# Hyena convolutions over even and odd pairs of positions, with half the matrix products, and weights whose low part a DMA adds up

## The chip, the cores and the metric

The kernel runs on one core of one Trainium2 chip. The core has a matrix engine (TensorE, PE in the rows), VectorE (DVE), ScalarE (ACT), GpSimd (POOL), SyncE (SP) and DMA engines that move data between HBM and the on-chip memory (SBUF). Matrix products are written to PSUM, eight banks of 128 x 512 floats. The metric is the time of one execution on the device in microseconds, the median of several runs. A profile is one execution taken by the hardware profiler.

## The reference, cut to what matters

One layer of an encoder: a combined input projection (2048 to 11264 columns), four groups of 1024 channels (convolution, Fourier mixing, Hyena long convolutions, attention over a memory), a gate, an output projection. The change is in the Hyena group:

```python
hy = depthwise_conv(hy, hy_short_w, hy_short_b)      # width 3
v, x1, x2 = jnp.split(hy, 3, axis=-1)
kf = hyena_filters(...)                              # spectra, (L+1, 2, 1024)
z = v
for o, g_o in enumerate((x1, x2)):
    z = g_o * long_conv(z, kf[:, o], hy_skip[o])     # zero-padded FFT convolution, L = 512
y_c = z
```

So there are 8 blocks of 128 channels with 2 long convolutions each, 16 in all; the second of a block takes the result of the first.

## The kernel before, in words

**Precision.** Every product is in float32 made from rounded parts. A matrix is split into a high part (rounded to fp32r) and a low part (what is left), and `mm3` (L102) issues three matmuls: high x high, high x low, low x high. `split` (L77) makes the parts: ScalarE copies the source into the high part (L79), VectorE subtracts it from the source (L80).

**Projection weights.** `project` (L304) computes one block of 128 output columns: 2 chunks of 1024 weights per partition, 24 matmuls of 512 columns each. `wload` (L98) loads a chunk (512 KB, from SyncE's queue) into `raw`, ScalarE writes `wh`, VectorE writes `wl`. `raw`, `wh` and `wl` have three buffers each, so the parts of a chunk can be written when the products of the chunk three earlier are done.

**The Hyena stage** (loop at L608). For each of 8 blocks `ct`: three projections with the short convolution (`short`, L535) give `v`, `x1` and `x2`; two `long_conv` (L546) follow; in four of the blocks there are also two projections for the convolution group (`conv_proj`) and 30 multiply-adds on VectorE over the positions (`conv_taps`, L516).

**One long convolution before.** Sums and differences of even positions and reversed odd positions (`pq`, L553 and L554), 4 transposes (L558), a split (`tH`, `tL`), the forward transform as products with two 256 x 256 tables (`mtab`; 24 matmuls of 256 columns), the product with the filter's spectrum (`kt_`, loaded from `kd`) as 4 multiplications and 2 sums on VectorE, two splits (`uH`, `uL`, `vH`, `vL`), the inverse transform (24 matmuls of 256 columns, that leave the positions on the free axis), scaling, skip term and gate.

**What sets the order.** The program is written with a tile framework: when it is built, a scheduler takes instructions by priority and by its own estimate of times and lays down one fixed order for each engine, so matmuls of the next projections stand between those of a convolution. On the chip each engine runs its list in order, and an instruction whose input or buffer isn't ready holds up all behind it. GpSimd's list has only additions (L476 for sums of squares, L520 for channel sums) in this stage.

Of the kernel before, what the change touches and what calls it, by code (L numbers as in the profile page):

```python
# [20 lines left out]
P = 128  # L21
# [21 lines left out]
def encoder_kernel(ctx: ExitStack, tc: tile.TileContext, a: dict, out: bass.AP):  # L43
# [26 lines left out]
    def pg():  # L70
        return psg.tile([P, 512], F32, tag="pg", name=nm("pg"))
# [463 lines left out]
    def short(b, j):  # L535
        ps = project(b)
# [6 lines left out]
    MH = [mtab[:, 0, i, :].rearrange("p (s r) -> p s r", s=2) for i in range(2)]  # L543
    ML = [mtab[:, 1, i, :].rearrange("p (s r) -> p s r", s=2) for i in range(2)]

    def long_conv(z, g, dst, o, ct):  # L546
# [17 lines left out]
        pu, px = pg(), pg()
        for m, pst in ((0, pu), (1, px)):
            for rt in range(2):
                o_ = pst[:, 256 * rt:256 * rt + 256]
                for st in range(2):
                    s = slice(P * rt, P * rt + P)
                    if m == 0:  # L570
                        xh, xl = tHv[:, st], tLv[:, st]
                    else:
                        xh, xl = tHv[:, st, ::-1, :], tLv[:, st, ::-1, :]
                    mm3(o_, MH[m][:, st, s], ML[m][:, st, s], xh, xl, st == 0, st == 1)
        puv = pu.rearrange("p (r c n) -> p r c n", r=2, c=2)
        pxv = px.rearrange("p (r c n) -> p r c n", r=2, c=2)
        kc, ks = kt_[:, :, 0:2, :], kt_[:, :, 2:4, :]
        uH, uL, vH, vL = (wt(t, (P, 2, 2, P), F32R, 1) for t in ("uH", "uL", "vH", "vL"))
        for yh, yl, k1, k2, op in ((uH, uL, kc, ks, add), (vH, vL, ks, kc, sub)):
            p1 = wt("pp", (P, 2, 2, P), bufs=3)  # L580
            p2 = wt("pp", (P, 2, 2, P), bufs=3)
            dve.tensor_tensor(p1, puv, k1, op=mul)
            dve.tensor_tensor(p2, pxv, k2, op=mul)
            if op == add:
                dve.tensor_tensor(p1, p1, p2, op=add)  # L585
            else:
                dve.tensor_tensor(p1, p2, p1, op=sub)
            split(yh, yl, p1)
        pd = pg()

        for f in range(2):
            o_ = pd[:, 256 * f:256 * f + 256]
            n = 0
            for m, yh, yl, c in ((0, uH, uL, f), (1, vH, vL, 1 - f)):
                for rt in range(2):
                    mm3(o_, yh[:, rt, c, :], yl[:, rt, c, :], MH[m][:, rt, :], ML[m][:, rt, :], n == 0, n == 3)
                    n += 1
        ci = cinv[:, o, ct:ct + 1]
        dsb = wt("dsb", (P, 256))
        act.activation(dsb, pd[:, 256:512], AF.Copy, scale=ci)  # L600
        yc = wt("yc")
# [6 lines left out]
    for ct in range(CT):  # L608
# [7 lines left out]
        group_square(y, gacc, wt("pp", (P, 2, 2, P), bufs=3).rearrange("p a b c -> p (a b c)"), ct == 0)  # L616
# [552 lines left out]
```

## Time and profile before

| | |
|---|---|
| median of 3 runs | 1731.67 us (1730.17 to 1737.29) |
| profiled execution | 1736.26 us, of which 1734.0 us from its first to its last instruction (the span) |
| TensorE busy | 1687.0 us, 97% of the span; granted clock 0.987 of 2.4 GHz on the mean |
| VectorE, ScalarE, GpSimd busy | 1205.5, 752.3 and 151.4 us |
| DMA | 215.13 MB, mean 124 GB/s |

A matmul's row gives its start and its length; the lengths overlap, so the rate of TensorE is read from the distance of the starts. "Idle before" is the time in which an engine stood still ahead of a group of instructions, with what ended it. The Hyena stage lies between about 320 and 790 us of the span.

### The profile page before, as it was taken

The numbers are of one execution on the slowest core, as the hardware profiler recorded it, in microseconds if no ns is written. First come the engines' busy times: TensorE is split into PE (matmuls) and PEld (weight loads), VectorE is DVE, ScalarE is ACT, GpSimd is POOL, SyncE is SP. The second block draws the span as 40 slices with busy tenths as digits, with TensorE's granted clock in tenths as the row PEclk, the third lists the DMA queues.
The fourth block names the chain that finished last, engine by engine and source line by source line (L and its number), as shares of the span: only waits on it lengthen the run. The fifth ranks groups of instructions, "written<-read, shape, count | busy, mean of one in ns | idle before, by whom it ended". The sixth has DMA issues, their size and how long they took to land.

```text
span 1734.0 us, 22272 instructions
## 1 busy us (share of the span) xinstructions
PE 1687.0 (97%) x8521; PEld 1424.7 (82%) x8521; DVE 1205.5 (70%) x1755; ACT 752.3 (43%) x1121; POOL 151.4 (9%) x98
## 2 busy tenths in 40 slices
PE   7999999999999999999999999999999699999997
PEld 5987888888888888888888898888878588888876
DVE  7966988478587686878765879986462545454586
ACT  6645655232223222223434346445453444444564
POOL 4201432000000000000000011100021100000000
PEclk9999999999999999999999999999999899999999
DMA  8654443432222322223333234232222523232355
GB/s 285 226 186 150 158 146 134 158 95 88 98 93 90 97 98 91 77 82 116 128 116 128 94 117 158 98 109 86 74 85 97 200 98 104 98 103 98 117 206 182
DMA packets 80575, 215.13 MB, mean 124 GB/s; under 512 B 8146, under 2 KB 25810, under 8 KB 79956
## 3 DMA queue, kind: packets, MB, share of 16 engines
q1 hardware_dynamic: 80468, 213.70, 36.5%
q8 instruction: 67, 1.10, 0.3%
q14 instruction: 40, 0.33, 0.1%
HBM read 195.05 MB, written 18.63 MB: 123 GB/s over the span
## 4 chain that ended last, share of the span: by engine, by line
PE 87%; DVE 7%; issue 2%; ACT 2%; DMA 2%; POOL 1%; SPq 0%; DVEq 0%; ACTq 0%; POOLq 0%
PE pf L105 16%; PE pf L103 16%; PE pf L104 16%; PE pg L103 12%; PE pg L104 12%; PE pg L105 12%; DVE y L516 2%; DVE wl L80 2%; DMA raw<-in_wv_dram 1%; POOL vacc L476 1%; ACT wh L79 1%; DMA kdm<-mst 0%; PE pg L558 0%; DVE y L491 0%; PE pg L411 0%
## 5 line engine op out<-in xcount | busy, mean ns | idle before, releaser
L103 PE MATMUL pf<-hH,wh 128*128 128x512 f32 x1280 | 504.7, 394 | 0.0
L105 PE MATMUL pf<-hH,wl 128*128 128x512 f32 x1280 | 502.1, 392 | 0.0
L104 PE MATMUL pf<-hL,wh 128*128 128x512 f32 x1280 | 501.5, 392 | 0.0
L80 DVE TENSOR_TENSOR wl<-raw,wh 128x1024 fp32r<-128x1024 f32 (+1 forms) x288 | 359.1, 1249 | 187.0 <-ACT wh L79 185.8
L79 ACT ACTIVATE wh<-raw 128x1024 fp32r<-128x1024 f32 (+1 forms) x288 | 298.3, 1037 | 358.9 <-PE pf L104 275.8
L103 PEld LDWEIGHTS pf<-hH,wh 128*128 128x128 f32 x1280 | 241.8, 189 | 47.7 <-issue 0.8
L105 PEld LDWEIGHTS pf<-hH,wl 128*128 128x128 f32 x1280 | 241.5, 189 | 47.4 <-issue 0.5
L104 PEld LDWEIGHTS pf<-hL,wh 128*128 128x128 f32 x1280 | 241.4, 189 | 47.2 <-issue 0.2
L80 DVE TENSOR_TENSOR jl<-y,jh 128x512 fp32r<-128x512 f32 (+1 forms) x154 | 91.5, 597 | 121.2 <-ACT jh L79 120.1
L79 ACT ACTIVATE jh<-y 128x512 fp32r<-128x512 f32 (+1 forms) x154 | 84.5, 550 | 179.3 <-PE pg L104 113.0
L103 PE MATMUL pg<-wh,jh 128*128 128x512 f32 x384 | 150.5, 392 | 11.2 <-ACT jh L79 11.2
L104 PE MATMUL pg<-wl,jh 128*128 128x512 f32 x384 | 150.2, 391 | 0.0
L105 PE MATMUL pg<-wh,jl 128*128 128x512 f32 x384 | 150.1, 391 | 0.0
L103 PEld LDWEIGHTS pg<-wh,jh 128*128 128x128 f32 x384 | 72.6, 189 | 26.4 <-ACT jh L79 11.5
L516 DVE SCALAR_TENSOR_TENSOR y<-ubuf,par,y 128x512 f32<-128x512 f32 x120 | 89.8, 748 | 2.5
L105 PEld LDWEIGHTS pg<-wh,jl 128*128 128x128 f32 x384 | 72.5, 189 | 15.4 <-DVE jl L80 0.2
L104 PEld LDWEIGHTS pg<-wl,jh 128*128 128x128 f32 x384 | 72.7, 189 | 15.1
L79 ACT ACTIVATE uH<-pp 128x512 fp32r<-128x512 f32 x16 | 10.1, 632 | 92.9 <-DVE pp L585 92.9
L516 DVE SCALAR_TENSOR_TENSOR y<-ub,par,y 128x512 f32<-128x512 f32 x60 | 46.4, 773 | 2.3 <-ACT y L514 1.1
L427 POOL TENSOR_TENSOR y<-fsq,y 128x512 f32<-128x512 f32 x24 | 43.6, 1815 | 41.5 <-ACT fsq L426 41.4
L104 PE MATMUL pf<-wl,jh 128*128 128x512 f32 x116 | 45.2, 390 | 1.3 <-DVE wl L80 1.3
L516 DVE SCALAR_TENSOR_TENSOR y<-ubm,par,y 128x512 f32<-128x512 f32 x60 | 45.2, 753 | 0.8
(374 smaller groups left out, 2847.3 us busy)
## 6 DMA issues: line engine op xcount, KB each, us to landing
raw<-in_w_std_dram SPq DMA_DIRECT2D x160, 512.0 KB, 3.8
raw<-in_wo_dram SPq DMA_DIRECT2D x77, 512.0 KB, 3.3
raw<-in_wk_dram SPq DMA_DIRECT2D x16, 512.0 KB, 4.0
kd<-y SPq DMA_DIRECT2D x16, 512.0 KB, 3.5
y<-kd SPq DMA_DIRECT2D x32, 256.0 KB, 3.3
raw<-in_w_f_dram SPq DMA_DIRECT2D x16, 512.0 KB, 3.3
raw<-in_wv_dram SPq DMA_DIRECT2D x15, 512.0 KB, 5.9
y<-in_xT_dram SPq DMA_DIRECT2D x8, 512.0 KB, 6.8
```

The costliest lines, as they stand in the source:

```text
L79: act.activation(h, src, AF.Copy)
L80: dve.tensor_tensor(l, src, h, op=sub)
L103: pe.matmul(ps, wh, xh, start=start, stop=False)
L104: pe.matmul(ps, wh, xl, start=False, stop=False)
L105: pe.matmul(ps, wl, xh, start=False, stop=stop)
L427: pool.tensor_tensor(acc, sq, acc, op=add)
L476: pool.tensor_tensor(acc, sqt, acc, op=add)
L516: dve.scalar_tensor_tensor(o, u[:, t:t + L], conv_w[:, ct, t:t + 1], o, op0=mul, op1=add)
```

## The change: what it does

- `long_conv`: the sums and differences `pq` are taken for even and odd pair indices apart (positions in steps of four), the forward transform uses two 128 x 128 tables for each of the two (12 matmuls of 256 columns), and sums and differences on VectorE build the full spectrum from the two halves. After the product with the filter the same is done backwards, then one split of 1024 elements (`wwH`, `wwL`) in place of two of 512, and 12 matmuls. The result lies with positions on the partitions, so 4 transposes (L624) turn it back. ScalarE copies one half out of PSUM at L584 and L617 and makes the skip term (L626).
- `short` takes its weights by `wload_dma`: ScalarE writes the negated rounded weights into `wl` and the rounded ones into `wh`, and a DMA from GpSimd's queue adds the same 512 KB of HBM onto `wl`. VectorE doesn't touch these chunks. 48 of the chunks are loaded in this way; those of `conv_proj` are as before.
- Several working tiles have one buffer where they had two. Tables change: `mtab` has other values, half the columns of `etab` are doubled, some with their sign turned.

```diff
+    def wload_dma(src):
+        raw = load(src)
+        h, l = wparts()
+        act.activation(l, raw, AF.Copy, scale=-1.0)
+        act.activation(h, raw, AF.Copy)
+        pool.dma_start(l, src, accum_op=add)
+        return h, l
...
-    def project(b, fill=None):
+    def project(b, fill=None, how=wload):
...
-            wh, wl = wload(a["w_std"][b, :, 1024 * c:1024 * c + 1024])
+            wh, wl = how(a["w_std"][b, :, 1024 * c:1024 * c + 1024])
...
-        ps = project(b)
+        ps = project(b, how=wload_dma)
...
-        for m, pst in ((0, pu), (1, px)):
-            for rt in range(2):
...
-                for st in range(2):
...
-                    mm3(o_, MH[m][:, st, s], ML[m][:, st, s], xh, xl, st == 0, st == 1)
+        for e in range(2):
+            v = slice(256 * e, 256 * e + 256)
+            for m in range(2):
+                mm3(pse[e][:, 256 * m:256 * m + 256], MH[:, 0, m, e], ML[:, 0, m, e], tH[:, v], tL[:, v], True, True)
+        odd = wt("pp", bufs=3)
+        act.activation(odd, pse[1], AF.Copy)
+        xy = wt("t1", bufs=1)
+        ab = wt("ab4", (P, 2, 2, 256), bufs=1)
+        dve.tensor_tensor(xy, pse[0], odd, op=add)
+        dve.tensor_tensor(ab[:, :, 1, :], pse[0].rearrange("p (m n) -> p m n", m=2), odd.rearrange("p (m n) -> p m n", m=2), op=sub)
+        dve.tensor_tensor(ab[:, 0, 0, :], xy[:, 0:256], xy[:, 256:512], op=add)
+        dve.tensor_tensor(ab[:, 1, 0, :], xy[:, 0:256], xy[:, 256:512], op=sub)
...
+            dve.tensor_tensor(p1, x1_, k1, op=mul)
+            dve.tensor_tensor(p2, x2_, k2, op=mul)
+            dve.tensor_tensor(uv[:, i_].rearrange("p r (c n) -> p r c n", c=2), p1, p2, op=op)
+        sd = wt("t1", (P, 2, 256), bufs=1)
+        dve.tensor_tensor(sd[:, 0], uv[:, 0, 0], uv[:, 1, 0], op=add)
+        dve.tensor_tensor(sd[:, 1], uv[:, 0, 0], uv[:, 1, 0], op=sub)
+        w_ = wt("ab4", (P, 2, 2, 256), bufs=1)
+        dve.tensor_tensor(w_[:, 0], sd, uv[:, :, 1, :], op=add)
+        dve.tensor_tensor(w_[:, 1], sd, uv[:, :, 1, :], op=sub)
...
+        split(wH, wL, w_)
         pd = pg()
+        for e in range(2):
+            for m in range(2):
+                mm3(pd[:, 256 * e:256 * e + 256], MH[:, 1, m, e], ML[:, 1, m, e], wH[:, e, m], wL[:, e, m], m == 0, m == 1)
...
+        act.activation(dif, pdv[:, 1], AF.Copy)
+        th_ = wt("t1", (P, 2, 2, P), bufs=1)
+        dve.tensor_tensor(th_[:, 0], pdv[:, 0], dif, op=add)
+        dve.tensor_tensor(th_[:, 1], pdv[:, 0], dif, op=sub)
+        pc = pg()
+        for h in range(2):
+            for e in range(2):
+                pe.transpose(pc[:, 256 * h + P * e:256 * h + P * e + P], th_[:, h, e, :], ident)
+        yc = wt("yc", bufs=1)
+        act.activation(yc, z, AF.Copy, scale=skip[:, o, ct:ct + 1])
+        pcv = pc.rearrange("p (h e n) -> p h e n", h=2, e=2)
+        for h, yv in enumerate(pairs(yc)):
+            dve.scalar_tensor_tensor(yv, pcv[:, h], cinv[:, o, ct:ct + 1], yv, op0=mul, op1=add)
         dve.tensor_tensor(dst, yc, g, op=mul)
```

Three places show how the order moves. The first is TensorE's list in the first long convolution, between the last matmul of the forward transform (into `pg_562`) and the first of the inverse. `pf` rows are matmuls of projections; before, the inverse takes `uH`, and 13 projection matmuls stand between:

```order
L105 MATMUL pg_562_3234<-tH_559_3229,mtab_3009 128x256
L104 MATMUL pf_593_3402<-hL_99,wh_595_3405 128x512
L105 MATMUL pf_593_3402<-hH_98,wl_596_3406 128x512
...
L103 MATMUL pf_593_3402<-hH_98,wh_598_3435 128x512
L104 MATMUL pf_593_3402<-hL_99,wh_598_3435 128x512
L103 MATMUL pg_571_3277<-mtab_3009,uH_563_3259 128x256
```

After, the inverse takes `wwH` and `wwL`, and 52 projection matmuls stand at the place of the 13:

```order
L114 MATMUL pg_562_3240<-tH_559_3235,mtab_3009 128x256
L113 MATMUL pf_605_3398<-hL_99,wh_607_3401 128x512
L114 MATMUL pf_605_3398<-hH_98,wl_608_3402 128x512
...
L112 MATMUL pf_612_3460<-hH_98,wh_614_3463 128x512
L113 MATMUL pf_612_3460<-hL_99,wh_614_3463 128x512
L112 MATMUL pg_575_3282<-wwH_573_3278,mtab_3009 128x256
```

In the 16 convolutions there are 43 to 62 projection matmuls at this place.

The second is VectorE's list between these same two points. Before, four multiplications (`pp` from PSUM), two sums and the splits:

```order
L582 TENSOR_TENSOR pp_567_3263<-pg_561_3233,y2_531_3018 128x512
L583 TENSOR_TENSOR pp_568_3264<-pg_562_3234,y2_531_3018 128x512
L582 TENSOR_TENSOR pp_569_3270<-pg_561_3233,y2_531_3018 128x512
...
L585 TENSOR_TENSOR pp_567_3263<-pp_567_3263,pp_568_3264 128x512
L583 TENSOR_TENSOR pp_570_3271<-pg_562_3234,y2_531_3018 128x512
```

After, 14 instructions stand between the forward transform and `wwH` (the first four and the last four of them, then the split's low part):

```order
L587 TENSOR_TENSOR t1_564_3255<-pg_561_3239,pp_563_3253 128x512
L588 TENSOR_TENSOR ab4_565_3256<-pg_561_3239,pp_563_3253 128x2x256
L589 TENSOR_TENSOR ab4_565_3256<-t1_564_3255 128x256
L590 TENSOR_TENSOR ab4_565_3256<-t1_564_3255 128x256
...
L602 TENSOR_TENSOR t1_571_3272<-uv_566_3261 128x256
L603 TENSOR_TENSOR t1_571_3272<-uv_566_3261 128x256
L605 TENSOR_TENSOR ab4_572_3275<-t1_571_3272,uv_566_3261 128x512
L606 TENSOR_TENSOR ab4_572_3275<-t1_571_3272,uv_566_3261 128x512
L80 TENSOR_TENSOR wwL_574_3279<-ab4_572_3275,wwH_573_3278 128x1024
```

The middle six are the four multiplications and two sums, as before in number and size.

The third is GpSimd's list in the middle of the stage, which before held additions alone and now has the 48 transfers among them:

```order
L108 DMA wl_709_4065<-in_w_std_dram 128x1024
L108 DMA wl_712_4096<-in_w_std_dram 128x1024
L485 TENSOR_TENSOR gaccC_3023<-pp_689_3924,gaccC_3023 128x512
L108 DMA wl_779_4462<-in_w_std_dram 128x1024
L108 DMA wl_782_4493<-in_w_std_dram 128x1024
```

## Rows read from the trace of the kernel before

**Rows 1.** The page: busy us, share of the span, instructions of an engine.

```profile
PE 1687.0 (97%) x8521; PEld 1424.7 (82%) x8521; DVE 1205.5 (70%) x1755; ACT 752.3 (43%) x1121; POOL 151.4 (9%) x98
```

**Rows 2.** Busy time of each engine in the Hyena stage, clock, DMA share, GB/s.

```profile
320.00:790.00 470.00, 469.99 (x2441) 394.09 (x2440) 347.09 (x493) 133.34 (x175) 17.10 (x10) 1.00 0.28 92
```

**Rows 3.** Groups on TensorE, 320 to 790 us: busy, mean ns, idle before.

```profile
L104 PE MATMUL pg<-tL,mtab 128*128 128x256 f32 x128 | 35.6, 284 | 0.0
...
L104 PE MATMUL pg<-mtab,vH 128*128 128x256 f32 x64 | 18.1, 282 | 0.0
...
L558 PE MATMUL pg<-ident,pq 128*128 128x128 f32 x64 | 11.1, 276 | 0.0
```

**Rows 4.** TensorE in order of time: start, length, instruction.

```profile
339.26 0.39 PE L105 MATMUL pf<-hH,wl 128*128 128x512 f32 x1
339.49 0.60 PE L558 MATMUL pg<-ident,pq 128*128 128x128 f32 x4
339.85 0.47 PE L103 MATMUL pf<-hH,wh 128*128 128x512 f32 x1
...
343.33 0.28 PE L105 MATMUL pg<-tH,mtab 128*128 128x256 f32 x1
...
345.73 0.28 PE L105 MATMUL pg<-tH,mtab 128*128 128x256 f32 x1
...
365.20 0.39 PE L103 MATMUL pf<-hH,wh 128*128 128x512 f32 x1
...
367.24 0.39 PE L103 MATMUL pf<-hH,wh 128*128 128x512 f32 x1
```

**Rows 5.** Groups on VectorE, 320 to 790 us.

```profile
L80 DVE TENSOR_TENSOR wl<-raw,wh 128x1024 fp32r<-128x1024 f32 x68 | 84.3, 1240 | 44.2 <-ACT wh L79 43.6
...
L582 DVE TENSOR_TENSOR pp<-pg,y 128x512 f32<-128x512 f32 x32 | 22.0, 686 | 17.4 <-PE pg L105 17.4
...
L602 DVE SCALAR_TENSOR_TENSOR yc<-pg,cinv,dsb 128x256 f32<-128x256 f32 x16 | 7.7, 484 | 46.1 <-ACT dsb L600 46.1
...
L553 DVE TENSOR_TENSOR pq<-vx 128x256 f32<-128x256 f32 x8 | 3.4, 422 | 0.1
```

**Rows 6.** Groups on ScalarE, 320 to 790 us.

```profile
L79 ACT ACTIVATE wh<-raw 128x1024 fp32r<-128x1024 f32 x67 | 70.9, 1058 | 169.3 <-PE pf L104 160.4 <-issue 8.8
...
L79 ACT ACTIVATE tH<-pg 128x512 fp32r<-128x512 f32 x16 | 9.5, 591 | 0.2
L600 ACT ACTIVATE dsb<-pg,cinv 128x256 f32<-128x256 f32 x16 | 7.6, 477 | 56.1 <-PE pg L105 56.1
```

**Rows 7.** Waits, 320 to 790 us: who for whom, total us, times, longest.

```profile
PEld pg L103 <- ACT vH L79: 4.1, 15, 0.3
PEld pg L103 <- ACT tH L79: 3.6, 16, 0.3
```

**Rows 8.** DMA, 320 to 790 us: queue's share; issues, KB each, us to landing.

```profile
q1 hardware_dynamic: 23733, 42.76, 27.5%
...
raw<-in_w_std_dram SPq DMA_DIRECT2D x65, 512.0 KB, 3.7
```

**Rows 9.** DMA, 0 to 60 us, the busiest stretch: the slowest 512 KB transfer.

```profile
y<-in_xT_dram SPq DMA_DIRECT2D x8, 512.0 KB, 6.8
```

**Rows 10.** GpSimd's additions: min/median/max ns, first and last start.

```profile
L476 POOL TENSOR_TENSOR gaccC<-pp,gaccC x7: 1296/1305/1764, 443.9 to 782.8; 128x512 f32<-128x512 f32 x7
...
L520 POOL TENSOR_TENSOR csum<-y,csum x6: 1292/2209/2877, 635.2 to 1180.2; 128x512 f32<-128x512 f32 x6
```

**Rows 11.** VectorE in order of time, with taps of the convolution group.

```profile
376.88 4.68 DVE L516 SCALAR_TENSOR_TENSOR y<-ubuf,par,y 128x512 f32<-128x512 f32 x6
381.48 1.22 DVE L80 TENSOR_TENSOR wl<-raw,wh 128x1024 fp32r<-128x1024 f32 x1
382.62 3.89 DVE L516 SCALAR_TENSOR_TENSOR y<-ubuf,par,y 128x512 f32<-128x512 f32 x5
```

More of the change, by code (lines that the diff above doesn't have):

```diff
@@ L541, in short, with pairs @@
         return t
-    MH = [mtab[:, 0, i, :].rearrange("p (s r) -> p s r", s=2) for i in range(2)]
-    ML = [mtab[:, 1, i, :].rearrange("p (s r) -> p s r", s=2) for i in range(2)]
+    MH, ML = (mtab[:, i].rearrange("p (d m e n) -> p d m e n", d=2, m=2, e=2) for i in range(2))
+    def pairs(z):
+        return z[:, 0::2].rearrange("p (i e) -> p e i", e=2), z[:, 511::-2].rearrange("p (i e) -> p e i", e=2)
     def long_conv(z, g, dst, o, ct):
@@ L551, in long_conv @@
             sp.dma_start(kt_[:, rt], kdr[ct // 2][o][:, rt, :, cs])
-        pq = wt("pq")
-        dve.tensor_tensor(pq[:, 0:256], z[:, 0::2], z[:, 511::-2], op=add)
-        dve.tensor_tensor(pq[:, 256:512], z[:, 0::2], z[:, 511::-2], op=sub)
+        z0, z1 = pairs(z)
+        pq = wt("pq", (P, 2, 2, P), bufs=1)
+        dve.tensor_tensor(pq[:, 0], z0, z1, op=add)
+        dve.tensor_tensor(pq[:, 1], z0, z1, op=sub)
         pt = pg()
-        for st in range(2):
+        for e in range(2):
@@ L564, in long_conv @@
-        pu, px = pg(), pg()
-        for m, pst in ((0, pu), (1, px)):
-            for rt in range(2):
[L567 to L573, printed above, removed]
-                    mm3(o_, MH[m][:, st, s], ML[m][:, st, s], xh, xl, st == 0, st == 1)
@@ L577, in long_conv @@
+        dve.tensor_tensor(xy, pse[0], odd, op=add)
+        dve.tensor_tensor(ab[:, :, 1, :], pse[0].rearrange("p (m n) -> p m n", m=2), odd.rearrange("p (m n) -> p m n", m=2), op=sub)
+        dve.tensor_tensor(ab[:, 0, 0, :], xy[:, 0:256], xy[:, 256:512], op=add)
+        dve.tensor_tensor(ab[:, 1, 0, :], xy[:, 0:256], xy[:, 256:512], op=sub)
+        av, bv = (ab[:, i_].rearrange("p r (c n) -> p r c n", c=2) for i_ in range(2))
         kc, ks = kt_[:, :, 0:2, :], kt_[:, :, 2:4, :]
-        uH, uL, vH, vL = (wt(t, (P, 2, 2, P), F32R, 1) for t in ("uH", "uL", "vH", "vL"))
@@ L579, in long_conv @@
-        for yh, yl, k1, k2, op in ((uH, uL, kc, ks, add), (vH, vL, ks, kc, sub)):
+        uv = wt("uv", (P, 2, 2, 256), bufs=1)
+        for i_, (x1_, k1, x2_, k2, op) in enumerate(((av, kc, bv[:, :, ::-1, :], ks, add), (bv, kc[:, :, ::-1, :], av[:, :, ::-1, :], ks[:, :, ::-1, :], sub))):
             p1 = wt("pp", (P, 2, 2, P), bufs=3)
             p2 = wt("pp", (P, 2, 2, P), bufs=3)
[L582 to L588, printed above, removed]
@@ L589, in long_conv @@
-        pd = pg()
[L591 to L601, printed above, removed]
@@ new lines, in long_conv @@
+        dve.tensor_tensor(sd[:, 0], uv[:, 0, 0], uv[:, 1, 0], op=add)
[3 more added lines that the diff above has]
+        dve.tensor_tensor(w_[:, 1], sd, uv[:, :, 1, :], op=sub)
+        wH = wt("wwH", (P, 2, 2, 256), F32R, 1)
+        wL = wt("wwL", (P, 2, 2, 256), F32R, 1)
+        split(wH, wL, w_)
+        pd = pg()
+        for e in range(2):
+            for m in range(2):
+                mm3(pd[:, 256 * e:256 * e + 256], MH[:, 1, m, e], ML[:, 1, m, e], wH[:, e, m], wL[:, e, m], m == 0, m == 1)
@@ new lines, in long_conv @@
+        pdv = pd.rearrange("p (e f n) -> p f e n", e=2, f=2)
+        dif = wt("pp", (P, 2, P), bufs=3)
+        act.activation(dif, pdv[:, 1], AF.Copy)
[4 more added lines that the diff above has]
+        for h in range(2):
+            for e in range(2):
+                pe.transpose(pc[:, 256 * h + P * e:256 * h + P * e + P], th_[:, h, e, :], ident)
@@ L1053, in _tables @@
     i = np.arange(256)
-    th = np.pi * np.outer(4 * i + 1, 4 * i + 1) / 2048.0
-    m = np.stack([np.cos(th) + np.sin(th), np.cos(th) - np.sin(th)])
-    t = {"mtab": m.reshape(2, 2, P, 256).transpose(2, 0, 1, 3).reshape(P, 1024)}
+    j = np.arange(P)
+    m = np.stack([np.stack([f(np.pi * np.outer(8 * j + 4 * e + 1, 4 * j + 1) / 2048.0) for e in range(2)]) for f in (np.cos, np.sin)])
+    t = {"mtab": np.stack([m.transpose(2, 0, 1, 3), m.transpose(3, 0, 1, 2)], axis=1).reshape(P, 1024)}
     phi = np.pi * (4 * i + 1) / 1024.0
     e = np.stack([f(np.outer(2 * i + par, phi)) for f in (np.cos, np.sin) for par in (0, 1)])
+    e[:2, :, P:] *= 2.0
+    e[2:, :, P:] *= -2.0
     t["etab"] = e.reshape(4, 2, P, 256).transpose(2, 0, 1, 3).reshape(P, 2048)
```

20 lines of the change are left out of this document (7 added, 13 removed).

## The prediction

> **What bounds the kernel now.** I read the page first: TensorE is busy for 97% of the span [rows 1], so the question is whether it also works without gaps in the stage that changes. The stretch of the Hyena stage, 320 to 790 us, answers it: TensorE is busy 469.99 of 470.00 us at the full clock (1.00), VectorE 347 us (74%), ScalarE 133 us (28%), GpSimd 17 us, and the DMA engines are in use for 28% [rows 2]. The groups on TensorE show no idle time before them [rows 3], and the waits of its weight loads for ScalarE or VectorE are short: at most 0.3 us each, 4.1 and 3.6 us in all 16 convolutions for the two longest kinds, most of it under a running matmul [rows 7]. So this stage lasts as long as the sum of its matmul steps, and a matmul less is its step less, as long as nothing else becomes late.
>
> **TensorE's sum.** Steps are distances of starts. Projection matmuls of 512 columns: from 365.20 to 367.24 lie 9 steps, 0.227 us each. Matmuls of 256 columns: from 343.33 to 345.73 lie 20 steps, 0.120 us each. Four transposes stand between two projection matmuls that start 0.59 us apart; less one step, 0.36 us, 0.09 us each [rows 4]. The convolutions have 768 matmuls of 256 columns (three lines of 128 forward, six of 64 inverse, one row of each kind shown [rows 3]); the change halves them: 384 x 0.120 = 46.1 us less. It adds 64 transposes, 64 x 0.09 = 5.8 us. Net -40.3 us. The number of projection matmuls stays.
>
> **VectorE.** Durations: 0.69 us for 512 elements, 0.42 for 256 (0.48 from PSUM), 1.24 for 1024 [rows 5]. One convolution gains four instructions of 512 (`xy`, one half of `ab`, two for `w_`: 2.76), four of 256 (1.69), two of 256 from PSUM (0.97), has one split of 1024 for two of 512 (1.24 - 1.37) and loses the skip term, of 512 (0.7; it goes to ScalarE): +4.5 us, 72 us in 16. The 48 subtractions for `wl` go: 48 x 1.24 = 59.5 us. VectorE thus ends with 347 + 13 = 360 us in a stage of about 434 us: 83%. It is not the bound on the mean.
>
> **ScalarE.** 48 more conversions at 1.06 us are 51 us [rows 6]; a convolution has two copies of 512 (0.59 each), one of 256 (0.48) and one of 1024 (1.06) where it had two of 512 and one of 256, about +1 us, 16 us in all. 133 + 67 = 200 us, 46%. No bound either, but it works its list in order, and a conversion that waits for a buffer holds up those behind it.
>
> **The convolution's chain.** From the end of the forward transform to the first inverse matmul lie a ScalarE copy (0.59), ten VectorE instructions of 512 and four of 256 (6.86 + 1.69) and ScalarE's copy into `wwH` (1.06): 10.2 us [rows 5, 6]. Where instructions follow each other, the next starts up to 0.08 us before the end of the one ahead (376.88 + 4.68 against 381.48 [rows 11]); 13 times that takes it down to 9.2. The order puts 43 to 62 projection matmuls there: 9.8 to 14.1 us at 0.227. At the tightest place the chain ends between 0.6 us too early and 0.4 us too late, plus the hand-overs between engines; at the others VectorE has other work in between. Each convolution also has one hand-over more than before (the turn back). The old order, made in the same way, cost next to nothing. I take 0.25 us for each convolution, 4 us in all; the ends are 0 and 0.6 us (10 us).
>
> **The weights by DMA.** The trace of before has no transfer that adds and none from GpSimd. `wl` of a chunk is free when the chunk three earlier is done and needed by the third matmul of its own: two chunks and two matmuls, 50 x 0.227 = 11.3 us at the tightest (11.3 to 14.9 in all but the first three, since convolution matmuls stand between). ScalarE needs two conversions, the first a matmul earlier: 2.1 - 0.2 = 1.9 us. So 9.4 us are left for GpSimd's issue and the transfer at the tightest place, 11 typically. The bounds of its time X: a plain load of the same 512 KB lands 3.7 us after its issue here [rows 8]; the slowest 512 KB transfer, in the busiest stretch, took 6.8 us [rows 9], and since the adding one has to read its destination as well, twice that, 13.6, is the upper end. I take twice the row of this stage, 7.4 us, which fits into 9.4: cost 0. What hides it is the projection matmuls of the two chunks before. The DMA engines carry 25 MB more on 43 [rows 8]: from 27.5% to some 47%, or 64% if the second read costs as much. Nothing comes free of idle by moving 59.5 us from VectorE, since TensorE didn't wait for it.
>
> What is late if X is too long: three buffers turn. An adding chunk holds its buffer for 5.4 (its 24 matmuls) + 1.9 + X, a plain one for 5.4 + 1.06 + 1.24 = 7.7. Two blocks, one of them with the convolution group, have 12 and 4 of these: (12 (X + 7.3) + 4 x 7.7) / 3 = 4X + 39.5 us. TensorE needs for them 16 x 5.44 + 4 x (24 x 0.12 + 8 x 0.09) = 101.4 us. They are equal at X = 15.5, and each us more costs 4 us in each of the four pairs, 16 us in all. At 13.6 the mean still fits, but single tight places run late by up to 4.2 us; a late chunk makes the next two easier, so some 5 us in a pair, 20 us in all.
>
> Behind a transfer on GpSimd stand the later transfers and 10 or so additions. An addition takes 1.3 to 2.2 us, rarely 2.9 [rows 10], and waits for ScalarE's squares or for the last tap; at the tightest place the margin of 9.4 - 7.4 = 2.0 us is about one addition.
>
> **A rule that speaks against it.** GpSimd's addition of 512 elements takes 1.31 us at the median in one group and 2.21 in another, the second right behind VectorE's taps [rows 10]; so the two engines do disturb each other in this kernel. The Trainium skill (SBUF — State Buffer, section "SBUF: two separate sides") says that GpSimd writes the descriptors of the DMAs that it issues, and can't while VectorE holds the pair of ports they share, which single-source float32 copies do; two-input instructions hold it only against reads by GpSimd. By that, the two-input instructions of this stage would not delay a transfer, and the sum stays; read more widely, it is the third rival below.
>
> **Sum.** -46.1 + 5.8 + 4 = -36.3 us. The profiled execution took 1736.26 us (1734.0 of it span), which gives 1700; it lay 4.6 us above the median of 1731.67, and from that the forecast is 1695.
>
> **Rivals.**
> 1. *Adding transfers turn too slowly (slower).* The only place where the change can lose more than it gains is the round of the three `wl` buffers. From X = 17.7 us the delay, 16 X - 248 us, eats the 36 us; at X = 20 it is 72 us, and the time 1732 - 36 + 72 = 1768. For it: no row shows such a transfer, and it is 4.8 times the plain one. Against: even the slowest plain one, doubled, stays at 13.6. Chance 0.12.
> 2. *The longer chain shows.* VectorE at 83% with taps and `wl` subtractions of the other projections in its list delivers `wwH` 1.5 us late in each convolution: 24 us in place of 4, 1715. For it: 43 matmuls cover barely 10.2 us, and 14 dependent steps stand where there were 4. Against: before, the same kind of order lost at most 0.3 us at a hand-over [rows 7]. The same time comes out if X is near 13 us. Chance 0.15.
> 3. *GpSimd can't issue while VectorE is busy (no change).* VectorE runs 9.6 us without a pause among the taps (376.88 to 386.51 [rows 11]). If the issue waits for the end of such a run, X is 7.4 + 9.6 = 17 there, 7.6 us too late, once or twice in each of the four blocks with taps: 30 to 61 us. That is 1726 to 1756, with 1731 as the likeliest, no gain. Chance 0.07.
>
> **How the numbers follow.** Forecast 0.66 (1688 to 1706: from 0 to 10 us of hand-overs, and some us of the runs' own spread), rivals 0.12, 0.15 and 0.07. A difference under 0.5%, 8.7 us, can't be told from no change. Faster by more than that (below 1723): the forecast, nearly all of rival 2: 0.80. Within it: most of rival 3 and a little of the others: 0.07. Slower (above 1740): rival 1 and a part of 3: 0.13. The range goes from 1687 to 1735; above it lies rival 1 and half of rival 3, some 0.16, below it 0.03. The forecast's own range is 1688 to 1706.
>
> **What would show it.** Right: in the stage (then some 434 us long) TensorE without idle time and at clock 1.00, 384 matmuls of 256 columns left of 768, 128 transposes, and `wl` transfers that land within 9 us of ScalarE's conversion. Wrong: `pf` matmuls with idle time released by the `wl` DMA (rivals 1 and 3; in 3 only beside taps), or `pg` matmuls with idle time released by `wwH`, `wwL` or `t1` (rival 2); or a clock below 1.00 in the stage, which would come from such pauses.

## The result, and the profile after

The changed kernel takes 1715.51 us in the median of 4 runs (1713.90 to 1717.04), the kernel before, on the same chip, 1733.12 us (1730.17 to 1737.29). The ratio is 0.9894, with a 95% interval of 0.9877 to 0.9911: 18 us less, half of the 36 us that were forecast. The profiled execution took 1716.29 us, 1714.5 of it span (1734.0 before).

The page's first line, in answer to [rows 1]: busy us, share of the span, instructions.

```profile
PE 1655.3 (97%) x8201; PEld 1386.6 (81%) x8201; DVE 1221.9 (71%) x1835; ACT 813.6 (47%) x1185; POOL 189.9 (11%) x146
```

TensorE's share of the span is 97% as before. The stage itself says more. Busy time, clock, DMA share and GB/s, in answer to [rows 2]:

```profile
320.00:766.00 446.00, 436.04 (x2109) 353.28 (x2108) 357.08 (x554) 186.73 (x228) 51.27 (x52) 1.00 0.63 150
...
500.00:600.00 100.00, 96.92 (x474) 77.79 (x472) 80.10 (x128) 41.57 (x52) 12.78 (x13) 1.00 0.66 152
```

TensorE stood idle for 10 of 446 us, where it was busy for 469.99 of 470; the pauses lie all over the stage, and the clock stays full in it. Starts show more than busy time does, since a row's length overlaps the next: from start to start, less the usual step (0.227, 0.120 or 0.091 us), TensorE lost 7.8 us between 300 and 795 us before the change and 24.8 us between 300 and 760 us after it. What it waited for stands in the waits (us in all, times, longest), in answer to [rows 7]:

```profile
PEld pg L113 <- DVE tL L80: 9.9, 14, 1.9
...
PE pg L113 <- DVE tL L80: 4.9, 6, 1.5
PEld pg L112 <- ACT wwH L79: 4.7, 15, 0.6
...
PE pg L573 <- DVE pq L568: 4.4, 8, 0.6
```

Two places cost: the transposes of `pq` (L573; 8.3 us by the starts) and the first matmul that needs `tL` (L113; 6.5 us). The place on which the prediction spent its argument, `wwH`, costs 1.0 us by the starts, most of its wait lying under running matmuls.

The turn from the first convolution of a block to the second, on TensorE and VectorE in order of time (start, length, instruction, idle before):

```profile
358.57 0.69 PE L624 MATMUL pg<-ident,t 128*128 128x128 f32 x4
359.01 0.48 PE L112 MATMUL pf<-hH,wh 128*128 128x512 f32 x1
...
359.30 1.29 DVE L629 SCALAR_TENSOR_TENSOR yc<-pg,cinv,yc 128x256 f32<-128x256 f32 x2 [0.53 <-PE pg L624]
...
360.62 0.69 DVE L630 TENSOR_TENSOR y<-yc,vx 128x512 f32<-128x512 f32 x1
...
361.17 0.39 PE L112 MATMUL pf<-hH,wh 128*128 128x512 f32 x1
361.35 0.63 DVE L568 TENSOR_TENSOR pq<-y 128x256 f32<-128x256 f32 x1
...
361.89 0.63 DVE L569 TENSOR_TENSOR pq<-y 128x256 f32<-128x256 f32 x1
...
362.03 0.33 PE L573 MATMUL pg<-ident,pq 128*128 128x128 f32 x1 [0.47 <-DVE pq L568]
362.11 0.48 PE L113 MATMUL pf<-hL,wh 128*128 128x512 f32 x1
362.58 0.55 PE L573 MATMUL pg<-ident,pq 128*128 128x128 f32 x3
```

VectorE works from 359.30 to 362.52 without a gap: it isn't waiting, its instructions last 3.2 us. TensorE has ten projection matmuls for that time, 2.27 us, and loses some 0.9 us at each of the eight such places. In the order before the change, 16 projection matmuls stood between two convolutions at each of these places, and the next transposes started 3.83 us after the last inverse matmul did: the new order also has less to cover this turn. In answer to [rows 5], VectorE's groups there (busy, mean ns of one, idle before):

```profile
L629 DVE SCALAR_TENSOR_TENSOR yc<-pg,cinv,yc 128x256 f32<-128x256 f32 x30 | 19.2, 688 | 6.5 <-PE pg L624 6.3
...
L589 DVE TENSOR_TENSOR ab<-t 128x256 f32<-128x256 f32 x16 | 6.7, 416 | 0.0
...
L568 DVE TENSOR_TENSOR pq<-y 128x256 f32<-128x256 f32 x8 | 5.0, 628 | 0.3
```

All three have 256 elements. `ab`, contiguous, takes 416 ns; `pq`, whose sources step by four floats, 628, where its ancestor with steps of two took 422 [rows 5]; `yc`, read and written in steps of four, 688 for 484.

The second place, in a block with taps:

```profile
510.18 0.49 PE L112 MATMUL pg<-tH,mtab 128*128 128x256 f32 x2
...
511.48 0.74 DVE L548 SCALAR_TENSOR_TENSOR vx<-pf,par,vx 128x511 f32<-128x511 f32 x1
...
512.81 0.74 DVE L549 SCALAR_TENSOR_TENSOR vx<-pf,par,vx 128x511 f32<-128x511 f32 x1
...
513.47 0.68 DVE L80 TENSOR_TENSOR tL<-pg,tH 128x512 fp32r<-128x512 f32 x1
...
514.20 0.39 PE L113 MATMUL pg<-tL,mtab 128*128 128x256 f32 x1 [1.46 <-DVE tL L80]
```

`tL` could start when `tH` was there (TensorE takes it at 510.18), but stands in VectorE's list behind taps and a short convolution that are themselves late. Three such pauses are 1.7 to 1.9 us long from start to start.

A third loss lies behind the stage, where the next one begins:

```profile
780.47 0.36 PE L112 MATMUL pg<-jh,wh 128*128 128x258 f32 x1 [1.21 <-issue]
...
786.04 0.39 PE L112 MATMUL pg<-jh,wh 128*128 128x258 f32 x1 [1.65 <-ACT wh L79]
```

From 10 us ahead of the first `jh` matmul to 26 us behind it the pauses (steps at least 0.15 us longer than usual) add up to 4.2 us; before, to 0.2.

The transfers, in answer to [rows 8], between 300 and 766 us:

```profile
q0 software_dynamic: 6586, 23.96, 27.9%
...
raw<-in_w_std_dram SPq DMA_DIRECT2D x67, 512.0 KB, 4.7
wl<-in_w_std_dram POOLq DMA_DIRECT2D x45, 512.0 KB, 7.8
```

An adding transfer lands 7.8 us after its issue at the median (6.7 to 9.7); in the whole stage TensorE's matmuls wait for one once, for 0.3 us. GpSimd began 47 of the 48 issues within 0.6 us of the end of ScalarE's conversion, the other 2.4 us after it.

### The profile page after: what moved, and what is told of

Its sections match the earlier page's. It is cut to its first block, busy times and chain, and to the rows that moved or that the text cites. A ratio compares the mean times of both kernels' runs of the same rounds, so it can differ in the third digit from the quotient of the medians.

```text
span 1714.5 us, 21887 instructions
## 1 busy us (share of the span) xinstructions
PE 1655.3 (97%) x8201; PEld 1386.6 (81%) x8201; DVE 1221.9 (71%) x1835; ACT 813.6 (47%) x1185; POOL 189.9 (11%) x146
## 4 chain that ended last, share of the span: by engine, by line
PE 78%; DVE 14%; DMA 2%; issue 2%; ACT 2%; POOL 1%; SPq 0%; DVEq 0%; ACTq 0%; POOLq 0%
PE pf L114 14%; PE pf L112 14%; PE pf L113 14%; PE pg L113 11%; PE pg L112 11%; PE pg L114 11%; DVE y L525 5%; DVE wl L80 2%; DVE yc L629 1%; DMA raw<-in_wv_dram 1%; POOL vacc L485 1%; ACT wh L79 1%; DMA wl<-in_w_std_dram 1%; DVE y L630 1%; DVE pq L568 1%
## 5 line engine op out<-in xcount | busy, mean ns | idle before, releaser
L113 PE MATMUL pf<-hL,wh 128*128 128x512 f32 x1280 | 502.1, 392 | 0.0
L80 DVE TENSOR_TENSOR wl<-raw,wh 128x1024 fp32r<-128x1024 f32 (+1 forms) x240 | 304.0, 1269 | 151.6 <-ACT wh L79 151.0
L79 ACT ACTIVATE wh<-raw 128x1024 fp32r<-128x1024 f32 (+1 forms) x240 | 247.5, 1033 | 231.3 <-PE pf L113 140.8
L113 PEld LDWEIGHTS pf<-hL,wh 128*128 128x128 f32 x1280 | 241.9, 189 | 46.9 <-issue 0.2
L113 PE MATMUL pg<-wl,jh 128*128 128x512 f32 x384 | 150.5, 392 | 0.0
L107 ACT ACTIVATE wh<-raw 128x1024 fp32r<-128x1024 f32 x48 | 51.0, 1061 | 99.8 <-PE pf L113 51.8
L113 PEld LDWEIGHTS pg<-wl,jh 128*128 128x128 f32 x384 | 72.7, 189 | 15.1
L108 POOL DMA_DIRECT2D wl<-in_w_std_dram x48 | 41.7, 870 | 286.2 <-ACT wl L106 274.3
L106 ACT ACTIVATE wl<-raw 128x1024 fp32r<-128x1024 f32 x48 | 50.2, 1046 | 0.0
L1016 POOL TENSOR_TENSOR xres<-xres,og 128x512 f32<-128x512 f32 x4 | 6.7, 1682 | 372.2 <-ACT og L1015 372.2
```

The source lines that it names most:

```text
L79: act.activation(h, src, AF.Copy)
L80: dve.tensor_tensor(l, src, h, op=sub)
L106: act.activation(l, raw, AF.Copy, scale=-1.0)
L107: act.activation(h, raw, AF.Copy)
L108: pool.dma_start(l, src, accum_op=add)
L113: pe.matmul(ps, wh, xl, start=False, stop=False)
```

## The experiments

The theory: VectorE pays for a step of 16 bytes, 0.21 us per 256 elements, four times in a convolution; this makes the chain between two convolutions longer than its cover. The rivals: the adding transfers disturb VectorE; or the chain has too many steps, whatever each lasts. Where an interval is given, it is that of the ratio to the kernel before, run on the same chip (medians 1733.2 to 1734.2 us).

**Contiguous halves (near_all, near_pq).** In `pairs` (near_all), or for the reads of `pq` alone (near_pq):

```diff
-        return z[:, 0::2].rearrange("p (i e) -> p e i", e=2), z[:, 511::-2].rearrange("p (i e) -> p e i", e=2)
+        return tuple(z[:, 256 * h:256 * h + 256].rearrange("p (e i) -> p e i", e=2) for h in range(2))
```

> Leaves out: the sums, differences and scaled sums of a convolution take their 512 positions from two contiguous halves in another order, not from steps of four floats, so the values are those of other positions. The order of instructions on every engine is that of the changed kernel. Theory (far steps): VectorE's four instructions of 256 elements with a step of 16 bytes per convolution (0.65 us for pq, 0.69 for yc in the changed kernel) fall to those of before, 0.42 and 0.48; that is 64 x 0.21 = 13.5 us of VectorE, and TensorE's pauses ahead of the second convolution's first transposes (8.3 us in all) shrink to about 2; the time is 8 to 13 us below the changed kernel's 1715.5, 1703 to 1708. Rival A (contention): the instructions are long because the adding transfers disturb VectorE; they stay at 0.63 to 0.69, and the time stays within 3 us of 1715. Rival B (the chain's number of steps and hand-overs is what is late, whatever each lasts): the instructions fall, the pauses stay above 6 us, 1712 to 1716.

> Leaves out: only the sums and differences pq read two contiguous halves in place of steps of four floats, so their values are those of other positions; all else and the order are the changed kernel's. Theory (far steps): pq falls from 0.64 to 0.42 us, 32 x 0.22 = 7 us of VectorE; of the chain ahead of the second convolution's transposes 0.44 of 0.9 us goes, 8 x 0.44 = 3.5 us, and up to 2 us more where VectorE is behind among the taps: 1710 to 1712. Rival A (contention): pq stays at 0.63 or more, 1714 to 1717. Rival B (number of steps): pq falls, the time doesn't, 1714 to 1716.

near_all: 1703.97 us, ratio 0.9825 (0.9811 to 0.9838). near_pq: 1710.40, 0.9866 (0.9851 to 0.9881). Both as the theory had it. VectorE's groups in near_all:

```profile
L629 DVE SCALAR_TENSOR_TENSOR yc<-pg,cinv,yc 128x256 f32<-128x256 f32 x32 | 14.0, 479 | 7.1 <-PE pg L624 6.8
...
L568 DVE TENSOR_TENSOR pq<-y 128x256 f32<-128x256 f32 x8 | 3.4, 425 | 0.3
```

The instructions are the same and stand in the same order; 12 us hang on their steps alone. Ahead of `pq` TensorE loses 2.4 us by the starts in place of 8.3, ahead of `tL` 2.0 in place of 6.5: the lateness there was mostly a consequence.

**Each half of the change alone (dma_alone, conv_alone).**

```diff
 dma_alone, in the kernel before:
-        ps = project(b)
+        ps = project(b, how=wload_dma)
 conv_alone, in the changed kernel:
-        ps = project(b, how=wload_dma)
+        ps = project(b)
```

> The kernel before, with the adding transfers for the weights of the Hyena stage as its only change. Theory (far steps and a chain too long for its cover cause all the pauses): TensorE was busy without a gap in the stage, so what VectorE saves (48 x 1.24 = 59.5 us) buys nothing and ScalarE's 51 us more are hidden: 1732, within 4 us. Rival (the adding transfers or the second conversion on ScalarE cause the pauses): TensorE shows 10 to 17 us of pauses ahead of pf matmuls, 1742 to 1749.

> The changed kernel with the weights of before: VectorE subtracts, no transfer adds. Theory: pq and yc last as long as with the transfers (0.63 to 0.69), VectorE gets 59.5 us more and is at 424 us of some 450, 94%, so TensorE waits for it more often: 1722 to 1740, 7 to 25 us above the changed kernel. Rival A (contention by the adding transfers): pq and yc fall to 0.42 and 0.48 without the transfers, and the time is 1700 to 1710. Rival B (the transfers matter for nothing, VectorE's load either): within 3 us of 1715.

dma_alone: 1733.69 us, ratio 1.0001 (0.9991 to 1.0010). conv_alone: 1737.68, 1.0017 (1.0008 to 1.0026). The stretch 320 to 790 us of dma_alone:

```profile
320.00:790.00 470.00, 469.61 (x2438) 392.95 (x2437) 301.18 (x450) 173.52 (x219) 50.17 (x53) 1.00 0.60 143
```

The transfers cost TensorE nothing, and taking 46 us from VectorE buys nothing as long as TensorE is the bound. In conv_alone they are missing:

```profile
320.00:790.00 470.00, 448.05 (x2122) 361.02 (x2121) 405.50 (x604) 148.25 (x188) 17.20 (x9) 0.97 0.28 92
```

VectorE is busy for 405 of 470 us, and `pq` takes 0.62 to 0.64 us without any such transfer, so that contention is not what makes it long. In its blocks with taps VectorE empties one of the projections' two PSUM buffers too late, or writes `wl` too late (two pauses of over 4 us, at 612 and 727 us), and TensorE stands still for up to 6.0 us:

```profile
500.10 0.77 PE L624 MATMUL pg<-ident,t 128*128 128x128 f32 x4 [0.44 <-DVE t L619]
506.87 0.76 PE L112 MATMUL pf<-hH,wh 128*128 128x512 f32 x1 [6.00 <-DVE vx L549]
```

So the two halves need each other: half the matmuls alone gain nothing, and with the transfers 22 us (1737.7 against 1715.5). Part of what conv_alone loses is the clock, which falls with its long pauses (0.97 on the mean of the stretch; the last section has the rows).

**The steps moved to TensorE (pe_in, pe_out, pe_both).** The positions are put in order by the transposes. pe_in:

```diff
-        z0, z1 = pairs(z)
-        pq = wt("pq", (P, 2, 2, P), bufs=1)
+        z0, z1 = z[:, 0::2], z[:, 511::-2]
+        pq = wt("pq", (P, 2, 256), bufs=1)
...
-                pe.transpose(..., pq[:, f, e, :], ident)
+                pe.transpose(..., pq[:, f, e::2], ident)
```

pe_out:

```diff
-                pe.transpose(pc[:, 256 * h + P * e:256 * h + P * e + P], th_[:, h, e, :], ident)
+                pe.transpose(pc[:, 511 - 2 * e::-4] if h else pc[:, 2 * e::4], th_[:, h, e, :], ident)
...
-        for h, yv in enumerate(pairs(yc)):
-            dve.scalar_tensor_tensor(yv, pcv[:, h], cinv[:, o, ct:ct + 1], yv, op0=mul, op1=add)
+        dve.scalar_tensor_tensor(yc, pc, cinv[:, o, ct:ct + 1], yc, op0=mul, op1=add)
```

> The changed kernel's results by another way: pq is made of steps of two floats (as before the change) and kept in pair order, and TensorE's transposes read every second of its 256 columns. The order on every engine is that of the changed kernel. Theory (far steps on VectorE): pq falls to 0.42 us and, as with contiguous halves, the time to 1708 to 1712, if a transpose that reads with a step of two costs TensorE no more. Rival (TensorE pays for the step): the 64 transposes take 0.2 in place of 0.1 us each, 6.4 us more, 1714 to 1717.

> The changed kernel's results by another way: the transposes that turn the result back write PSUM with a step of four floats, to the positions where the values belong, and one VectorE instruction of 512 contiguous elements takes the place of two of 256 with steps. Theory (far steps on VectorE): 2 x 0.69 becomes 0.75, 16 x 0.63 = 10 us of VectorE; 0.6 us less on the chain ahead of the second convolution's transposes, 8 x 0.6 = 5 us, and 1 to 3 us of the pauses ahead of tL: 1707 to 1711. Rival (TensorE pays for its stepped writes): the 64 transposes take 0.1 to 0.2 us more each, 6 to 13 us: 1715 to 1722.

> Both of the steps moved from VectorE to TensorE's transposes, with the changed kernel's results. Theory: VectorE saves 16 x (0.44 + 0.63) = 17 us, more than with contiguous halves (13.5), so TensorE's pauses ahead of the first transposes and of tL fall to some 4 us together: 1701 to 1705. Rival (TensorE pays for the steps): 128 transposes longer by 0.1 us each eat 13 us: 1714 to 1718.

1710.34 (ratio 0.9848 to 0.9883), 1708.75 (0.9838 to 0.9868) and 1705.14 us (0.9817 to 0.9846): each in its range or 0.1 us beside it, and TensorE pays next to nothing. In pe_in, four transposes that read in steps of two floats take 0.385 us from the first start to the start of the next matmul, in place of 0.355: 0.5 us in all 64. In pe_out the four transposes that write PSUM in steps of four floats are 0.45 us ahead of the matmul behind them, as are the contiguous ones in the changed kernel above (0.44):

```profile
357.66 0.69 PE L624 MATMUL pg<-ident,t 128*128 128x128 f32 x4
358.11 0.48 PE L112 MATMUL pf<-hH,wh 128*128 128x512 f32 x1
```

VectorE in pe_both: one instruction of 512 elements does what took two.

```profile
L629 DVE SCALAR_TENSOR_TENSOR yc<-pg,cinv,yc 128x512 f32<-128x512 f32 x16 | 12.0, 751 | 8.6 <-PE pg L624 8.6
...
L568 DVE TENSOR_TENSOR pq<-y 128x256 f32<-128x256 f32 x8 | 3.4, 426 | 0.3
```

**A longer cover (cover15).** Edges that only set TensorE's order put the transposes of a second convolution behind later projection matmuls:

```diff
+    for n_, (u_, i_) in LATE.items():
+        for t_ in turn[4 * n_:4 * n_ + 4]:
+            tc.add_manual_dep(t_.ins, plog[u_][i_].ins.name, ...)
```

> The changed kernel with another order on TensorE: 15 to 17 projection matmuls in place of 10 between a first convolution's last transposes and the second's first. No instruction is added or cheaper. Theory (a chain of 2 x 0.69 + 0.69 + 2 x 0.64 = 3.35 us behind a cover of 10 x 0.227 = 2.27 us): 15 x 0.227 = 3.4 us cover it, the pause of 0.9 us at each of 8 places goes, 7 us, though pq and yc last as long as ever; the pauses ahead of tL stay: 1707 to 1711. Rival (VectorE has too much to do, whatever the order): what is gained there is lost at the next hand-over, 1713 to 1717.

1712.01 us, ratio 0.9873 (0.9856 to 0.9889): 1 us above the range, and too near to the changed kernel's 0.9894 for its intervals to part them. The trace shows what the theory says of the place (line numbers are one higher here):

```profile
PEld pg L114 <- DVE tL L81: 10.1, 15, 1.6
...
PE pg L114 <- DVE tL L81: 4.7, 8, 1.2
...
PEld pg L574 <- DVE pq L570: 0.7, 4, 0.2
```

The waits for `pq` are all but gone (1.1 us by the starts), with `pq` at 0.64 to 0.65 us, no shorter than before the edit; those for `tL` stay. The pauses in the stage fall by 7.1 us, the span by 6.3, the median by 3.5.

**How the price goes with the step (steps).** The halves ascending, with 1, 2, 4 or 8 floats from element to element in two channel blocks each:

```diff
+        return tuple(z[:, 256 * h:256 * h + 256].rearrange("p (j e) -> p e j", e=STEP[0]) for h in range(2))
```

> Leaves out: as with the contiguous halves, the values are those of other positions. The changed kernel with its order on every engine; pq and yc take their 256 elements contiguous in channel blocks 0 and 1, with a step of 2 floats in 2 and 3, of 4 in 4 and 5, of 8 in 6 and 7, always ascending. One look, for durations. Theory (the step in bytes sets the price): pq 0.42 us with a step of 1 and 2 floats, 0.64 with 4, and with 8 either 0.64 (a fixed price) or about 0.85 (the price goes on with the step); yc 0.48, 0.48, 0.69, and with 8 alike. Rival (the descending half or the three-dimensional pattern is what costs, not the step): 0.42 and 0.48 in all blocks.

One run (1715.57 us). The row of the second convolutions' `pq` sums in four stretches, one for each step (340 to 430, 430 to 540, 560 to 650, 665 to 766 us); behind the last two rows stands that of `yc` in the same stretch:

```profile
L568 DVE TENSOR_TENSOR pq<-y 128x256 f32<-128x256 f32 x2 | 0.8, 424 | 0.1
...
L568 DVE TENSOR_TENSOR pq<-y 128x256 f32<-128x256 f32 x2 | 0.8, 424 | 0.1
...
L568 DVE TENSOR_TENSOR pq<-y 128x256 f32<-128x256 f32 x2 | 1.2, 620 | 0.1
...
L629 DVE SCALAR_TENSOR_TENSOR yc<-pg,cinv,yc 128x256 f32<-128x256 f32 x6 | 3.8, 683 | 1.1 <-PE pg L624 1.1
...
L568 DVE TENSOR_TENSOR pq<-y 128x256 f32<-128x256 f32 x2 | 1.2, 621 | 0.1
...
L629 DVE SCALAR_TENSOR_TENSOR yc<-pg,cinv,yc 128x256 f32<-128x256 f32 x6 | 4.1, 738 | 1.2 <-PE pg L624 1.1
```

This row has 0.42 us at 4 and at 8 bytes, 0.62 at 16 and at 32. `yc` has 0.48, 0.48, 0.68 and 0.74, and the first convolutions' `pq` 0.42, 0.42, 0.62 and 0.68. So the price comes somewhere between 8 and 16 bytes, and in ascending halves too: it isn't the direction. Most of it is there at 16 bytes; whether it then stays fixed the run leaves open, since at 32 bytes one row is the same and the two others are 0.06 us longer.

**`tL` needed later (tl_last, on pe_both; tl_last_only, on the changed kernel).**

```diff
-        for e in range(2):
-            v = slice(256 * e, 256 * e + 256)
-            for m in range(2):
-                mm3(pse[e][:, 256 * m:256 * m + 256], MH[:, 0, m, e], ML[:, 0, m, e], tH[:, v], tL[:, v], True, True)
+        for part, x_ in ((MH, tH), (ML, tH), (MH, tL)):
+            for e in range(2):
+                for m in range(2):
+                    pe.matmul(pse[e][:, 256 * m:256 * m + 256], part[:, 0, m, e], x_[:, 256 * e:256 * e + 256], ...)
```

> The kernel with both steps moved to TensorE's transposes, with the forward transform's matmuls in another sequence: the eight that need only tH first, the four with tL last, so 8 x 0.12 = 0.96 us of work lie between (as built, up to 0.24 and some projection matmuls). Theory (tL is late because VectorE has the short convolution and taps ahead of it in its list, by up to 1.2 us in three blocks): those three pauses shrink to about 0.3 us, 2.7 us less: 1701 to 1704. Rival (the wait only moves to the next step of VectorE's list): 1704 to 1707.

> The changed kernel with the forward transform's matmuls in the other sequence alone (the eight that need tH first, the four with tL last); pq and yc keep their steps of four floats on VectorE. Theory (two causes that add up: the steps make the chain ahead of the second transposes too long for its cover, 8.3 us of pauses; tL is needed 0.12 us after tH, 6.5 us of pauses): the pauses ahead of tL go to about 1 us, those ahead of pq stay near 8, and what TensorE waits at the next stage's start (5 us) falls by up to 3: 1706 to 1711. Rival (the steps are the only cause, tL is late only as their consequence, and VectorE's list gives the time back at the next hand-over): 1713 to 1717.

tl_last: 1698.30 us, ratio 0.9799 (0.9785 to 0.9812), 17 us faster than the changed kernel and the best of all. tl_last_only: 1710.53, 0.9867 (0.9841 to 0.9892), as the theory had it. In tl_last TensorE is busy for 445.75 of 446 us (by the starts it still loses some 12 us, about half of the changed kernel's 24.8 and above the 7.8 of before), and the waits for `tL` are

```profile
PEld pg L582 <- DVE tL L80: 0.6, 1, 0.6
...
PE pg L582 <- DVE tL L80: 0.2, 1, 0.2
```

In tl_last_only `tL` costs 2.0 us by the starts (6.5 before that edit) and `pq` still 8.1: two places, each with its own remedy. tl_last is 3 us better than expected. In it the pauses at the next stage's start fall from 4.2 to 1.3 us; they do not in tl_last_only (4.2), so the order alone doesn't explain it.

**Both, and the last square elsewhere (best).**

```diff
-        group_square(y, gacc, wt("pp", bufs=3), ct == 0)
+        group_square(y, gacc, sgtile() if ct == CT - 1 else wt("pp", bufs=3), ct == 0)
```

> In addition to the kernel with the matmuls on tL last: 11 to 13 projection matmuls ahead of a second convolution's first transposes (10 before), and the last square of the stage is written to a tile that doesn't belong to the stage, so that the next stage's first sums wait no longer for GpSimd's addition (2.1 us). Theory: 0.5 to 1 us for the cover, since there the pauses are almost gone, and 1 to 3 us at the next stage's start, where TensorE pauses 4.6 us in all: 1699 to 1703. Rival (the start of the next stage hangs on VectorE's own list, not on the addition): as the kernel with tL last, within 1.5 us.

1718.24 us, ratio 0.9915 (0.9901 to 0.9930): a miss, 20 us slower than the kernel it was built on. The edges and the other tile changed the plan of the end of the stage; no projection matmuls were left there to lie beside the last convolution. TensorE in order of time, then the stretch 760 to 765 us (columns as in the windows above):

```profile
743.00 0.64 PE L583 MATMUL pg<-tL,mtab 128*128 128x256 f32 x4
753.45 0.58 PE L113 MATMUL pg<-wwH,mtab 128*128 128x256 f32 x1 [9.80 <-ACT wwH L80]
...
764.18 0.80 PE L113 MATMUL pf<-hH,wh 128*128 128x512 f32 x1 [4.66 <-ACT sgt L371]
...
760.00:765.00 5.00, 0.82 (x2) 0.72 (x3) 4.93 (x11) 1.95 (x4) 1.65 (x1) 0.50 0.01 2
```

The first gap is the bare chain from the forward to the inverse transform, 9.8 us of idle: close to the 9.2 to 10.2 us of the prediction. The second comes from the square's new tile: `sgt` has one buffer, into which ScalarE also copies projections out of PSUM (L371), so that copy and the projection behind it wait for the square and for GpSimd's addition. And the granted clock, 1.00 up to 740 us, is 0.50 (1.2 GHz) from 755 to 765, so the matmuls between the gaps run at the lower level. The next stage's start, for which the square was moved, does lose only 0.2 us here. But 96 projection matmuls now stand between the last convolution and that start, where tl_last has 43, so this isn't shown to be the square's doing; neither edit was run alone.

## Why the prediction was wrong: a sum that held and hand-overs that did not

The forecast was 1695 us, its own range 1688 to 1706; the time is 1715.5. The step that failed is the term for the hand-overs, +4 us, where the runs showed 21: at a place that the prediction didn't look at, and partly through two kinds of instructions, `pq` and `yc`, whose price it left as it was.

- **TensorE's sum** holds. Steps are still 0.120 and 0.227 us; half of the 768 matmuls are gone. The 128 transposes take 13.0 us between their starts in place of 5.3 for 64, so 7.7 us more, not 5.8; these 1.9 us stand among the pauses below, which are counted with 0.091 us for each transpose.
- **The adding transfers** cost nothing, as forecast: 7.8 us where 7.4 was taken, and dma_alone is equal to before. Rivals 1 and 3 fell. GpSimd issued one in 0.87 us in this stage, beside a VectorE at 80%, and 47 of 48 within 0.6 us of the conversion that they waited for; the narrower reading of the Trainium skill's rule (SBUF — State Buffer, section "SBUF: two separate sides"), that two-input instructions don't delay it, is the one that fits.
- **VectorE's and ScalarE's totals** hold: 357 us where 360 were forecast, and 187 us where 200 were. VectorE's is partly luck: added up row by row, its durations rose by 30.5 us over the whole kernel, where +13 was forecast for the stage; but its rows overlap, and busy time, which counts an overlap once, rose by 16.4 (1205.5 to 1221.9). A mean of 80% didn't say that it would be in time.
- **VectorE's prices: one was put at nothing.** The prediction's list of what a convolution gains leaves `pq` and `yc` out, as if they cost what they did: 0.42 and 0.48 us [rows 5], with steps of two floats. With steps of four they cost 0.63 and 0.69: 0.84 us in a convolution, 13.5 in 16. The Trainium skill has a rule on this that was not weighed (SBUF — State Buffer, section "Specifications (TRN2)"): full speed needs two hits or more in a 16-byte line, which float32 values 16 bytes apart don't give. The runs agree, with 0.42 us at 8 bytes and 0.62 or more at 16 and 32.
- **The hand-overs are the term that was mis-sized**: +4 us forecast. TensorE's pauses rose by 17.0 us in the stage (24.8 - 7.8) and by 4.0 at the start of the next. -40.3 + 17.0 + 4.0 = -19.3; the span fell by 19.5. (17.0 has in it the 1.9 us of the transposes.) The bounds (0 to 10 us) were drawn at the one place with the longest chain, forward to inverse, which has 43 to 62 matmuls of cover and costs 1 us. Unseen was the turn from one convolution to the next: the order has ten projection matmuls there, 2.27 us, and even with the rows' own prices for steps of two the chain `yc`, `yc`, `y`, `pq`, `pq` is 2 x 0.48 + 0.69 + 2 x 0.42 = 2.5 us (2.2 with the overlaps of 0.08 that the prediction saw), with no margin left. With steps of four it lasts 3.2.
- **Rival 2** had the engine (VectorE), but not the place: not `wwH`, but `pq` and `tL`. That its time was 1715 is luck. Its reason, more dependent instructions, is only part: with the same instructions on contiguous operands the time is 1704.
- With the steps on TensorE and `tL` last the forecast's time is nearly reached, by another kernel than the one forecast: 1698.3 us.

Left open in part: the next stage's start, which loses 1.3 us in tl_last, 0.2 in best and 3.7 to 4.7 in all other variants of the changed kernel. Its preparation stands behind the last convolution on VectorE and ScalarE, and the runs point at cover once more: with 96 to 112 projection matmuls between the last convolution and the first `jh` matmul (the kernel before, dma_alone, best) the start loses 0.2 us, with 30 to 43 (all others) 1.3 to 4.7. No run changes this number alone, and why tl_last with 43 loses less than conv_alone with 43 (4.4) stays open.

The single buffers of `pq`, `tH`, `tL` and others are a rival that no run tests alone. VectorE waits 1.9 us in all for `pq`'s buffer in the changed kernel (3 times); near_all and tl_last keep the single buffers and are 12 and 17 us faster, so what they can still cost lies in the rest.

## What to carry to other kernels

For every place where TensorE hands over to another engine and takes back, set the chain's instructions, each at the price of its own access pattern, against the matmuls that the order puts there; the place where the cover is shorter than its chain decides, not the longest chain or the mean load. An instruction whose float32 operands step by 16 bytes is not the one that steps by 8: look for a row with the same step, and where data must be reordered, let a transpose that is there anyway read or write the steps. A gain on TensorE may need relief on VectorE to show at all, and that relief may be worth nothing by itself: measure the halves apart.

## What the runs showed of the hardware

- VectorE, float32, two inputs from SBUF, 256 elements: 0.42 us with steps of 4 and 8 bytes, 0.62 with 16, 0.62 to 0.68 with 32; with one input from PSUM and the stepped one and the output in SBUF 0.48, 0.48, 0.68 and 0.74 (steps).
- TensorE's transposes wrote PSUM in steps of 16 bytes, also descending, as fast as contiguously: four in 0.45 and in 0.44 us, with a median of 0.11 us between starts in both. The Trainium skill (PSUM — Partial Sum Buffer, section "Specifications (TRN2)") says that a non-contiguous pattern slows matmuls significantly; these writes do not show it, and the measurement decides here.
- An adding transfer of 512 KB from GpSimd's queue: 7.8 us from issue to landing at the median, beside plain loads of the same size that took 4.7 in the same stretch (3.7 before [rows 8]).
- The granted clock stayed at 1.00 through the pauses of up to 1.9 us in the changed kernel's Hyena stage. Behind the stage, after the pauses that end at 780.47 and 786.04 us, it was 0.63 on the mean of 786 to 790 us, a mixture of the two levels (first row). In conv_alone, after the pause of 6.0 us at 500 to 507 us, it was 0.50 (1.2 GHz) for the next 6 us (the other rows; columns as in the windows above):

```profile
786.00:790.00 4.00, 3.96 (x22) 3.96 (x23) 3.61 (x10) 0.66 (x2) 0.00 (x0) 0.63 0.37 127
...
490.00:500.00 10.00, 8.91 (x44) 6.84 (x42) 9.91 (x18) 4.23 (x5) 0.00 (x0) 1.00 0.18 52
507.00:510.00 3.00, 2.49 (x5) 1.50 (x6) 3.00 (x4) 0.00 (x0) 0.00 (x0) 0.50 0.08 15
510.00:513.00 3.00, 3.00 (x8) 2.31 (x7) 3.00 (x6) 0.00 (x0) 0.00 (x0) 0.50 0.82 268
```
